# Attention biases gathered on the host, eight weight buffers, and norm chunks one group earlier in a two-layer diffusion backbone

## The chip, the cores and the metric

The kernel runs on one core of a Trainium2 chip. The metric is the device time of one execution in microseconds. The time before is the median of three runs, 2124.17 us (2123.88 to 2127.73).

A core has TensorE (PE in the profile; PEld are its weight loads), VectorE (DVE), ScalarE (ACT), GpSimd (POOL) and SyncE (SP), which here issues all DMAs. Each engine works through its own instructions in the order in which they were emitted, and semaphores order them between engines.

## The reference, cut to what matters

256 latent tokens and 256 context tokens of 1024 channels pass through two layers: half-step SwiGLU, a mixer, half-step SwiGLU, each after an RMSNorm with a learned shift and scale. The mixer projects to neighbourhood attention (8 heads), a Fourier mix and a windowed attention (8 heads, 2 key heads, a sink), and merges the three through gates. The second layer is computed for the latent tokens alone, where that suffices. The part that the change is about:

```python
dr_idx = key_rows - r[:, None] + NA_WIN_R - 1
dc_idx = jnp.clip(kcb - q_cols[..., None], -(NA_WIN_C - 1), NA_WIN_C - 1) + NA_WIN_C - 1
bias = bias_tab[:, dr_idx[:, None, None, :, None], dc_idx[None, :, :, None, :]]
...
s_loc = jnp.einsum('brcqhd,brcwkhd->bhrcqwk', qg, kb).astype(jnp.float32) * scale + bias[None]
s_loc = jnp.where(in_win[:, :, None, :], s_loc, NEG_INF)
```

The grid has 4 rows of 64 columns. A latent query sees all rows and 16 of the columns, with a bias by head, row distance and column distance, and besides all context keys without a bias. A context query sees the context keys alone.

## The kernel before, in words

Everything is held with channels along the 128 partitions. A product is one 128x128 weight block against a tile of 256 or 512 tokens, made of three matmuls in a reduced-precision form (`mm3`, L289 to L291): high half of the weights by high and low half of the tokens, then low half of the weights by the high half of the tokens. Order on every engine is the order of the program text (`manual_schedule`).

**Weights.** `Weights` streams 424 tiles of 8 products (128x1024, 512 KB) in a fixed order. A tile goes through a raw buffer (5 of them, loaded at L58), a high half written by ScalarE (`wh`, L67) and a low half, raw less high, written by VectorE or GpSimd (`wl`, L76). High and low halves share the pool `w` with 6 buffers, that is three tiles. `next` hands out one product. At the first product of tile n it emits the high half of tile n+2 (`ahead` is 2 after the first FFN group), and at the fifth the low half of n+2.

**Norms.** `Norm.chunks(k)` emits steps up to k+1. A step takes 128 channels of 256 tokens: VectorE multiplies (L206), ScalarE adds the shift and writes the high half (L208), and one step later VectorE writes the low half (L214). `first` in `ffn` is the first group of an FFN: it runs over k, emits `norm.chunks`, and multiplies the chunk with four weight blocks. With 512 tokens it does so in two passes of 256. The very first norm of the program (`norm.ready`) has steps of its own (`_first`, L221 to L229). The norm before the mixer is emitted from `fourier`, with its own calls. "The turn" is the place where one sublayer's last projection gives way to the next sublayer's norm and first group.

**Neighbourhood bias.** Eight tiles of the pool `act` (`nab`, two sets of four) hold biases for a pair of heads: 2 heads by 2 query halves, each 128 queries by 256 latent keys, with zeros behind for the 256 context keys (`memset` at L444). `na_bias_load` (L707) fills a set with eight DMAs that read a padded table in HBM with overlapping strides, in rows of 64 elements. `na_bias` (L711) adds the column mask on GpSimd, four adds a set. The set of pair 0 is loaded in `mix_loads`, at the end of the FFN before; it is masked, and pair 1 loaded, at the start of `mix`; the others follow at the end of each latent block (`after`, `bias_ahead`). `wa_mask` holds the windowed attention's band and 256 zeros, which also serve blocks without a mask.

**Attention.** `attention` runs a pipeline over blocks of four score tiles (128 queries by 512 keys, or 256 keys for context queries): scores (L726, L727), `weights` (L733: VectorE adds the mask and takes the row minimum of the negated sum; L735: ScalarE's exponential with its row sum), normalising (L752), transposes (L757), their split into high (L759, ScalarE) and low half (L764, VectorE), and the values (L775). Between the steps `fill` emits products of the projections that later blocks need, by due times (`DUES`). What these produce is split and moved between partitions by SyncE's DMAs: `stack` (L884) for queries and keys, L903 for the rotary embedding, with four or eight issues each. Of layer 0 there are 16 blocks, of layer 1 there are 8.

**The pool `act`** of 66 slots (2 KB a partition) holds all tiles of tokens: high and low halves, temporaries, scores. A tile's slot is reused when its last reader is done.

Of the kernel before, what the change touches and what calls it, by code (L numbers as in the profile page):

```python
# [14 lines left out]
KD = D // 128  # L15
DEPTH = 2
# [10 lines left out]
WINDOW = 128  # L27
BIAS_W = 2 * GRID_W - 1
O_NA_Q, O_NA_K, O_NA_V, O_FN, O_WA_Q, O_WA_K, O_WA_V, O_GATE = (
# [4 lines left out]
N_SUB = 424  # L34
N_ACT = 66
TAIL = 3
# [223 lines left out]
class Emit:  # L260
    def __init__(self, ctx, tc, d):
        self.tc, self.nc, self.d = tc, tc.nc, d
        pool = lambda name, bufs, **k: ctx.enter_context(tc.tile_pool(name=name, bufs=bufs, **k))
        self.const = pool("const", 1)
        self.act_p = pool("act", N_ACT)
        self.raw_p = pool("raw", 5)
        self.w_p = pool("w", 6)
        self.mod_p = pool("mod", 2)
        self.sm_p = pool("sm", 4)
        self.ps_p = pool("ps", 8, space=PSUM)  # L270
        self.W = Weights(self.nc, d["ws"], self.raw_p, self.w_p)
        self.mod = {}
# [90 lines left out]
    def setup(self):  # L363
# [55 lines left out]
        self.sin = c.tile([128, NLAT], F32, name="sin")  # L419
        self.na_mask = c.tile([128, NLAT], F32, name="na_mask")  # L420
        self.wa_mask = c.tile([128, 2, NT], F32, name="wa_mask")
        self.sink = c.tile([128, DEPTH, 4, 4], F32, name="sink")
# [3 lines left out]
    def setup_mix(self):  # L426
        nc, d = self.nc, self.d
        nc.sync.dma_start(out=self.g_fin, in_=d["g_final"])
        nc.sync.dma_start(out=self.cos, in_=d["cos"])
        nc.sync.dma_start(out=self.sin, in_=d["sin"])  # L430
        nc.sync.dma_start(out=self.na_mask, in_=d["na_mask"])
        nc.sync.dma_start(out=self.wa_mask, in_=d["wa_mask"])
        nc.sync.dma_start(out=self.sink, in_=d["sink"].partition_broadcast(128))
        yield
        nc.gpsimd.tensor_scalar(out=self.nsink, in0=self.sink, scalar1=-1.0, scalar2=None, op0=ALU.mult)

    def mix_loads(self, l):

        self.raw_dft = [self.tmp() for _ in range(2)]
        self.nc.sync.dma_start(out=self.raw_dft[0], in_=self.d["dft_n"])  # L440
        self.nc.sync.dma_start(out=self.raw_dft[1][:, :256], in_=self.d["dft_d"])
        self.nab = [[self.tmp() for _ in range(4)] for _ in range(2)]
        for t in self.nab[0] + self.nab[1]:
            self.nc.gpsimd.memset(t[:, NLAT:], 0.0)  # L444
        self.na_bias_load(l, 0)


# [60 lines left out]
    def ffn(self, l, which, n, norm, nxt):  # L508
# [12 lines left out]
        def first(passes):  # L521
# [3 lines left out]
            for vs in passes:  # L525
                lo, hi = 256 * vs[0], 256 * (vs[-1] + 1)
                for k in range(KD):
                    norm.chunks(vs[0] * KD + k)
                    if norm.ready:
# [164 lines left out]
    def na_bias_load(self, l, p):  # L694


        nc = self.nc
        tab = self.d["na_bias"]
        for i in range(4):
            t4 = self.nab[p % 2][i][:, :NLAT].rearrange("p (r c) -> p r c", c=GRID_W)  # L700
            hp, qt = divmod(i, 2)
            for r2 in range(2):
                first = WIN_R - 1 - (2 * qt + r2)
                off = ((l * 8 + 2 * p + hp) * GRID_W * (2 * WIN_R - 1) + first) * BIAS_W + GRID_W - 1
                src = bass.AP(tensor=tab.tensor, offset=tab.offset + off,
                              ap=[[(2 * WIN_R - 1) * BIAS_W - 1, GRID_W], [BIAS_W, ROWS], [1, GRID_W]])
                nc.sync.dma_start(out=t4[r2 * 64:r2 * 64 + 64], in_=src)  # L707

    def na_bias(self, p):
        for t in self.nab[p % 2]:  # L710
            self.nc.gpsimd.tensor_tensor(out=t[:, :NLAT], in0=t[:, :NLAT], in1=self.na_mask, op=ALU.add)  # L711

    def attention(self, makers, fill):
# [16 lines left out]
        def weights(b, i, ps):  # L730
            nk = len(b["kc"]) * 128
            e, nm = self.tmp(), b["nm"][:, i:i + 1]
            nc.vector.tensor_tensor_reduce(out=e[:, :nk], in0=ps, in1=b["mask"][i], scale=-1.0,  # L733
                                           scalar=b["init"][i], op0=ALU.add, op1=ALU.min, accum_out=nm)
# [109 lines left out]
    def mix(self, l, norm, nxt):  # L844
# [7 lines left out]
        if l == 0:  # L852
            next(self.mix_setup, None)
        self.na_bias(0)
        self.na_bias_load(l, 1)
        v_na = [self.split_heads(ps) for ps in self.project_rows(
# [143 lines left out]
        o_na, o_wa = [], []  # L1000
        zero = self.wa_mask[:, 0, NLAT:]

        def bias_ahead(p):
            self.na_bias(p)
            if p < 3:
                self.na_bias_load(l, p + 1)

# [14 lines left out]
        def na_block(p, lat):  # L1022
            def make():
                if lat:
                    o_na.append(self.tmp())
                return dict(q=ready(("nq", p)), k=ready(("nk", p)), q0=0 if lat else NLAT, o=o_na[p], sink=None,
                            kc=[0, 1, 2, 3] if lat else [2, 3], init=[3e38] * 4, left=left(o_na, p, lat),
                            after=(lambda: bias_ahead(p + 1)) if lat and p < 3 else None,
                            mask=self.nab[p % 2] if lat else [zero] * 4,
                            v=lambda kc, hp: v_na[kc][p // 2][:, (p % 2 * 2 + hp) * 128:(p % 2 * 2 + hp + 1) * 128])  # L1030
            return make

        def wa_block(p, lat):
            def make():
                if lat:
# [4 lines left out]
                            init=[self.nsink[:, l, p, i:i + 1] for i in range(4)],  # L1040
                            mask=[self.wa_mask[:, i % 2, :] for i in range(4)] if lat else [zero] * 4,
                            v=lambda kc, hp: v[kc // 2][:, (kc % 2 * 2 + hp) * 128:(kc % 2 * 2 + hp + 1) * 128])
# [87 lines left out]
def constants():  # L1130
# [6 lines left out]
    cos, sin = np.cos(ang).T, np.sin(ang).T  # L1137
    c = np.arange(GRID_W)
    start = np.clip(c - WIN_C // 2, 0, GRID_W - WIN_C)
    inside = (c[None] >= start[:, None]) & (c[None] < start[:, None] + WIN_C)  # L1140
    na = np.where(inside, 0.0, NEG).astype(f)
    band = np.where(np.abs(t[:, None] - t[None]) <= WINDOW, 0.0, NEG).astype(f).reshape(2, 128, NLAT)
    wa = np.concatenate([band, np.zeros((2, 128, NCTX), f)], -1).transpose(1, 0, 2)
    ang_n = 2 * np.pi * (np.outer(t, t) % NLAT) / NLAT
# [9 lines left out]
        "sin": np.concatenate([-sin, sin] * 2, 0),  # L1154
        "na_mask": np.tile(na, (2, ROWS)),
        "wa_mask": wa,
        "dft_n": dft_n,
# [4 lines left out]
def pack(inputs, order):  # L1162
# [67 lines left out]
```

## Time and profile before

| | |
|---|---|
| profiled execution | 2120.81 us, span 2119.0 us |
| three runs | 2124.17 us median (2123.88 to 2127.73) |
| mean granted TensorE clock | 0.992 |
| instructions | 29168 |
| ScalarE's high halves (L67) | 424 of 1056 ns |
| VectorE's low halves (L76) | 379 of 1254 ns |
| GpSimd's low halves (L76) | 45 of 2461 ns |
| bias loads (L707) | 64 issues of 64 KB, 2.7 us to landing |
| mask adds (L711) | 32, 25.2 us of GpSimd |
| HBM read | 305.99 MB, 145 GB/s over the span |

The profile is of one execution. Busy time counts an engine's instructions, not the waits of its queue. "Idle before" an instruction is the time that its engine stood, with what ended it. A wait for several things is put down to the one that came last. The share of busy time is an average over the program, so the stretch in which an engine stands is looked at by itself.

### The profile page before, as it was taken

To read this page: it belongs to the slowest core of one execution; us is meant where nothing else is said; L and a number is where in the kernel's file an instruction comes from. 1 tells how busy PE (TensorE), PEld (TensorE's weight loads), DVE (VectorE), ACT (ScalarE), POOL (GpSimd) and SP (SyncE) were. 2 spreads that over 40 slices of the span, in tenths; PEclk is the share of its full clock that TensorE was granted. 3 is DMA by queue.
4 is the path that set the end of the run, shared out by engine and by line. 5 is a ranking of instruction groups with operands and counts; after the bars stand their busy time and mean duration, and the time that the engine had idled before them with its cause. 6 is when DMAs were issued, how large, how long until landed. Compare 5 with 4: busy or idle time off the path is not lost. (4 is left out here: it accounts for less than half of the span.)

```text
span 2119.0 us, 29168 instructions
## 1 busy us (share of the span) xinstructions
PE 2050.9 (97%) x11193; PEld 1764.7 (83%) x11193; DVE 1283.7 (61%) x2035; ACT 848.5 (40%) x1362; POOL 355.7 (17%) x285
## 2 busy tenths in 40 slices
PE   7899999999999999999999989999999989999998
PEld 3688888878888888988888788888888878999998
DVE  6777776566675334687777465533336548566554
ACT  4422222345786222432222243222324458545443
POOL 4200000403441112300000220000012155330002
PEclk9999999999999999999999999999999999999999
DMA  7465566455532333466666545623344563554663
GB/s 271 139 199 182 196 199 212 124 152 144 136 85 73 100 92 98 150 186 193 199 189 200 186 143 186 199 90 100 99 112 145 145 177 110 160 179 153 186 181 109
DMA packets 119412, 327.05 MB, mean 154 GB/s; under 512 B 30692, under 2 KB 35940, under 8 KB 119272
## 3 DMA queue, kind: packets, MB, share of 16 engines
q1 hardware_dynamic: 119272, 325.18, 50.3%
q8 instruction: 88, 1.44, 0.3%
q14 instruction: 52, 0.43, 0.1%
HBM read 305.99 MB, written 1.05 MB: 145 GB/s over the span
## 5 line engine op out<-in xcount | busy, mean ns | idle before, releaser
L290 PE MATMUL ps<-act,wh 128*128 128x512 f32 (+1 forms) x3227 | 1120.9, 347 | 24.1 <-DVE act L229 13.6
L289 PE MATMUL ps<-act,wh 128*128 128x512 f32 (+1 forms) x3227 | 1121.3, 347 | 3.4 <-ACT act L298 1.9
L291 PE MATMUL ps<-act,wl 128*128 128x512 f32 (+1 forms) x3227 | 1118.9, 347 | 1.8 <-DVE wl L76 1.8
L67 ACT ACTIVATE wh<-raw 128x1024 fp32r<-128x1024 f32 x424 | 447.4, 1056 | 707.8 <-PE ps L290 573.7
L290 PEld LDWEIGHTS ps<-act,wh 128*128 128x128 f32 x3227 | 613.2, 190 | 101.8 <-DVE act L229 14.8
L289 PEld LDWEIGHTS ps<-act,wh 128*128 128x128 f32 x3227 | 613.1, 190 | 78.9 <-ACT act L298 2.5
L291 PEld LDWEIGHTS ps<-act,wl 128*128 128x128 f32 x3227 | 613.1, 190 | 77.9 <-DVE wl L76 2.9
L76 DVE TENSOR_TENSOR wl<-raw,wh 128x1024 fp32r<-128x1024 f32 x379 | 474.6, 1254 | 273.6 <-ACT wh L67 273.0
L311 DVE CUSTOM_DVE_ANT_0 dump<-ada,silu_row 128x1024 bf16<-128x1024 f32 x224 | 273.3, 1220 | 13.9 <-DMA ada<-in_w_ada 11.5
L298 ACT ACTIVATE act<-tmp 128x512 fp32r<-128x512 f32 (+1 forms) x122 | 66.9, 566 | 275.2 <-DVE tmp L516 261.8
L471 DVE SCALAR_TENSOR_TENSOR h<-ps,mod,h 128x256 f32<-128x256 f32 x136 | 61.7, 480 | 150.8 <-PE ps L291 150.8
L76 POOL TENSOR_TENSOR wl<-raw,wh 128x1024 fp32r<-128x1024 f32 x45 | 110.7, 2461 | 222.9 <-ACT wh L67 199.7
L454 POOL TENSOR_TENSOR tmp<-h 128x512 f32<-128x512 f32 (+1 forms) x7 | 11.6, 1661 | 782.3 <-DVE h L471 639.8
L516 DVE TENSOR_TENSOR tmp<-tmp,ps 128x512 f32<-128x512 f32 (+1 forms) x88 | 54.6, 621 | 112.1 <-PE ps L291 107.5
L299 DVE TENSOR_TENSOR act<-tmp,act 128x512 fp32r<-128x512 f32 (+1 forms) x122 | 74.3, 625 | 62.2 <-ACT act L298 62.2
L764 DVE TENSOR_TENSOR act<-ps,act 128x512 fp32r<-128x512 f32 x80 | 54.8, 685 | 35.8 <-ACT act L759 27.6
L735 ACT ACTIVATE tmp<-tmp,sm 128x512 f32<-128x512 f32 (+1 forms) x96 | 62.2, 648 | 32.8 <-DVE sm L733 31.5
L775 PE MATMUL ps<-act 128*128 128x256 f32 x320 | 63.0, 309 | 12.4 <-DVE act L764 11.2
L460 POOL TENSOR_TENSOR tmp<-h 128x256 f32<-128x256 f32 (+1 forms) x44 | 51.7, 1174 | 117.8 <-DVE h L471 112.9
L759 ACT ACTIVATE act<-ps 128x512 fp32r<-128x512 f32 x80 | 47.5, 593 | 39.9 <-PE ps L757 34.5
L444 POOL MEMSET tmp<- 128x256 f32 x16 | 4.8, 312 | 348.6 <-PE ps L291 347.9
L775 PEld LDWEIGHTS ps<-act 128*128 128x128 f32 x320 | 44.8, 189 | 17.5 <-DVE act L764 15.0
(110 smaller groups left out, 1372.8 us busy)
## 6 DMA issues: line engine op xcount, KB each, us to landing
raw<-in_ws SPq DMA_DIRECT2D x424, 512.0 KB, 3.7
ada<-in_w_ada SPq DMA_DIRECT2D x128, 512.0 KB, 3.9
act<-act SPq DMA_DIRECT2D x112, 128.0 KB, 2.3
tmp<-in_w_ada_sc SPq DMA_DIRECT2D x16, 256.0 KB, 5.2
tmp<-in_w_ada SPq DMA_DIRECT2D x16, 256.0 KB, 6.0
tmp<-in_na_bias SPq DMA_DIRECT2D x64, 64.0 KB, 2.7
h<-in_h SPq DMA_DIRECT2D x8, 256.0 KB, 5.2
act<-act SPq DMA_DIRECT2D x32, 64.0 KB, 2.0
```

The costliest lines, as they stand in the source:

```text
L67: self.nc.scalar.activation(out=wh, in_=self.raw[i], func=AF.Copy)
L76: self.lo_engine.tensor_tensor(out=wl, in0=self.raw.pop(i), in1=self.hi[i].bitcast(F32), op=ALU.subtract)
L289: mm(ps, lhsT=w[0], rhs=x[0], start=start, stop=False)
L290: mm(ps, lhsT=w[0], rhs=x[1], start=False, stop=False)
L291: mm(ps, lhsT=w[1], rhs=x[0], start=False, stop=stop)
L298: nc.scalar.activation(out=hi, in_=src, func=AF.Copy)
L299: nc.vector.tensor_tensor(out=lo, in0=src, in1=hi.bitcast(F32), op=ALU.subtract)
L311: self.nc.vector.tensor_tensor_reduce(out=self.dump[:, ks], in0=w, in1=self.silu_row[:, v, ks], scale=1.0, scalar=m if half else 0.0, op0= ...
L471: self.nc.vector.scalar_tensor_tensor(out=h, in0=ps, scalar=self.mod[l, g][:, v, j:j + 1], in1=h, op0=ALU.mult, op1=ALU.add)
L735: nc.scalar.activation(out=e[:, :nk], in_=e[:, :nk], func=AF.Exp, scale=-1.0, bias=nm, accum_out=b["sum"][:, i:i + 1])
L764: nc.vector.tensor_tensor(out=t[1], in0=ps, in1=t[0].bitcast(F32), op=ALU.subtract)
L775: nc.tensor.matmul(b["ps"][hp][:, :256], lhsT=v, rhs=t[j][:, cs], start=c == 0 and j == 0, stop=c == n - 1 and j == 1)
```

## The change

It does four things.

1. The biases are gathered on the host for each layer and pair of heads, with the column mask already in them, as 128 partitions by 4 tiles by 256 keys. A load is one DMA of 512 KB with 4 KB a partition.
2. One constant tile `masks` of 11 blocks of 256 keys takes the place of `nab`, `na_mask` and `wa_mask`: blocks 0 to 3 and 4 to 7 are the two bias sets, 8 and 9 the band of the windowed attention, 10 is zeros. A score tile of 512 keys reads its own block and block 10 with one strided view. The pairs 0 and 1 are both loaded in `mix_loads`, the pairs 2 and 3 after the blocks of 0 and 1. The adds of the column mask and the memsets are gone, and one memset of block 10 is added at the start.
3. The pool `w` has 8 buffers instead of 6, the pool `act` 60 instead of 66.
4. In `first`, `norm.chunks` is called for one k further, except in the program's first norm.

```diff
-N_ACT = 66
+N_ACT = 60
...
-        self.w_p = pool("w", 6)
+        self.w_p = pool("w", 8)
...
-        self.na_mask = c.tile([128, NLAT], F32, name="na_mask")
-        self.wa_mask = c.tile([128, 2, NT], F32, name="wa_mask")
+        self.masks = c.tile([128, 11, NLAT], F32, name="masks")
+        nc.gpsimd.memset(self.masks[:, 10, :], 0.0)
...
-        nc.sync.dma_start(out=self.na_mask, in_=d["na_mask"])
-        nc.sync.dma_start(out=self.wa_mask, in_=d["wa_mask"])
+        nc.sync.dma_start(out=self.masks[:, 8:10, :], in_=d["wa_mask"])
...
-        self.nab = [[self.tmp() for _ in range(4)] for _ in range(2)]
-        for t in self.nab[0] + self.nab[1]:
-            self.nc.gpsimd.memset(t[:, NLAT:], 0.0)
         self.na_bias_load(l, 0)
+        self.na_bias_load(l, 1)
...
-                    norm.chunks(vs[0] * KD + k)
+                    norm.chunks(vs[0] * KD + k + (not norm.ready))
...
     def na_bias_load(self, l, p):
...
+        self.nc.sync.dma_start(out=self.masks[:, p % 2 * 4:p % 2 * 4 + 4, :], in_=self.d["na_bias"][l, p])
...
-            nc.vector.tensor_tensor_reduce(out=e[:, :nk], in0=ps, in1=b["mask"][i], scale=-1.0,
+            m = b["mask"][i]
+            two = lambda t: t.rearrange("p (a k) -> p a k", k=NLAT)
+            blocks = (self.masks[:, m:m + 1, :] if nk == NLAT else self.masks[:, m:11:10 - m, :])
+            nc.vector.tensor_tensor_reduce(out=two(e[:, :nk]), in0=two(ps), in1=blocks, scale=-1.0,
                                            scalar=b["init"][i], op0=ALU.add, op1=ALU.min, accum_out=nm)
...
-        self.na_bias(0)
-        self.na_bias_load(l, 1)
...
-                            after=(lambda: bias_ahead(p + 1)) if lat and p < 3 else None,
-                            mask=self.nab[p % 2] if lat else [zero] * 4,
+                            after=(lambda: self.na_bias_load(l, p + 2)) if lat and p < 2 else None,
+                            mask=[p % 2 * 4 + i if lat else 10 for i in range(4)],
...
-                            mask=[self.wa_mask[:, i % 2, :] for i in range(4)] if lat else [zero] * 4,
+                            mask=[8 + i % 2 if lat else 10 for i in range(4)],
```

The rest of the diff is the packing of the inputs on the host, which is outside the time.

More of the change, by code (lines that the diff above doesn't have):

```diff
@@ L27 @@
 WINDOW = 128
-BIAS_W = 2 * GRID_W - 1
 O_NA_Q, O_NA_K, O_NA_V, O_FN, O_WA_Q, O_WA_K, O_WA_V, O_GATE = (
@@ L694, in na_bias_load @@
     def na_bias_load(self, l, p):
[L697 to L711, printed above, removed]
+        self.nc.sync.dma_start(out=self.masks[:, p % 2 * 4:p % 2 * 4 + 4, :], in_=self.d["na_bias"][l, p])
     def attention(self, makers, fill):
@@ L1000, in mix @@
         o_na, o_wa = [], []
[L1001 to L1006, printed above, removed]
         def split_out(o, p):
@@ L1137, in constants @@
     cos, sin = np.cos(ang).T, np.sin(ang).T
[L1138 to L1141, printed above, removed]
     band = np.where(np.abs(t[:, None] - t[None]) <= WINDOW, 0.0, NEG).astype(f).reshape(2, 128, NLAT)
-    wa = np.concatenate([band, np.zeros((2, 128, NCTX), f)], -1).transpose(1, 0, 2)
     ang_n = 2 * np.pi * (np.outer(t, t) % NLAT) / NLAT
@@ L1154, in constants @@
         "sin": np.concatenate([-sin, sin] * 2, 0),
-        "na_mask": np.tile(na, (2, ROWS)),
-        "wa_mask": wa,
+        "wa_mask": band.transpose(1, 0, 2),
         "dft_n": dft_n,
@@ L1175, in pack @@
     a["w_ada_sc"] = w["w_ada"][0, :, D:2 * D].reshape(KD, 128, 2, 512).transpose(2, 0, 1, 3)
-    pad = GRID_W - WIN_C
-    t = np.pad(w["na_bias"], ((0, 0), (0, 0), (0, 0), (pad, pad)))
-    a["na_bias"] = np.broadcast_to(t[:, :, None], t.shape[:2] + (GRID_W,) + t.shape[2:])
+    c, t = np.arange(GRID_W), np.arange(NLAT)
+    start = np.clip(c - WIN_C // 2, 0, GRID_W - WIN_C)
+    inside = (c[None] >= start[:, None]) & (c[None] < start[:, None] + WIN_C)
+    row, col = t // GRID_W, t % GRID_W
+    dr = row[None] - row[:, None] + WIN_R - 1
+    dc = np.clip(col[None] - col[:, None], 1 - WIN_C, WIN_C - 1) + WIN_C - 1
+    b = np.full((DEPTH, 8, NLAT, NLAT), NEG, np.float32)
+    inside = np.tile(inside, (ROWS, ROWS))
+    b[:, :, inside] = w["na_bias"][:, :, dr[inside], dc[inside]]
+    a["na_bias"] = b.reshape(DEPTH, 4, 2, 2, 128, NLAT).transpose(0, 1, 4, 2, 3, 5).reshape(DEPTH, 4, 128, 4, NLAT)
     s = w["wa_sink"]
@@ L1209 @@
     "c": (128, KD, 2), "b_ada": (128, DEPTH, 9, KD), "gains": (128, DEPTH, 3, 8), "g_final": (128, 8),
-    "na_bias": (DEPTH, 8, GRID_W, 2 * WIN_R - 1, BIAS_W), "sink": (DEPTH, 4, 4), "ident": (128, 128),
-    "cos": (128, NLAT), "sin": (128, NLAT), "na_mask": (128, NLAT), "wa_mask": (128, 2, NT),
+    "na_bias": (DEPTH, 4, 128, 4, NLAT), "sink": (DEPTH, 4, 4), "ident": (128, 128),
+    "cos": (128, NLAT), "sin": (128, NLAT), "wa_mask": (128, 2, NLAT),
     "dft_n": (128, 2 * NLAT), "dft_d": (128, 256),
```

## The prediction

> **What bounds the kernel now.** I read the page's busy times first, then a table of stretches, then what TensorE waited for, then the timeline at each place where it stood still.
>
> ```profile
> PE 2050.9 (97%) x11193; PEld 1764.7 (83%) x11193; DVE 1283.7 (61%) x2035; ACT 848.5 (40%) x1362; POOL 355.7 (17%) x285
> ```
>
> TensorE is busy 2050.9 us; nothing in this change removes a matmul, so only its idle time, and time at a lower clock, can be won. The stretches show where that lies (columns: length, then busy us and count by engine, granted clock, DMA share):
>
> ```profile
> core 0 of [0], span 2119.0 us
> core 0: us, PE busy (x) PEld busy (x) DVE busy (x) ACT busy (x) POOL busy (x), PEclk, DMA share, GB/s
> 20.00:75.00 55.00, 37.12 (x127) 23.15 (x128) 46.27 (x82) 25.49 (x44) 32.81 (x17) 0.84 0.48 176
> 415.00:446.00 31.00, 28.38 (x141) 22.43 (x140) 26.45 (x47) 18.49 (x29) 5.13 (x7) 1.00 0.54 155
> 510.00:690.00 180.00, 174.78 (x964) 147.76 (x963) 119.31 (x294) 131.47 (x316) 67.30 (x55) 1.00 0.40 107
> 1245.00:1278.00 33.00, 25.27 (x195) 23.93 (x196) 20.66 (x36) 15.06 (x23) 0.00 (x0) 1.00 0.48 144
> 1615.00:1632.00 17.00, 14.44 (x78) 11.69 (x77) 13.62 (x24) 8.60 (x15) 3.88 (x5) 1.00 0.46 135
> 1692.00:1726.00 34.00, 27.35 (x151) 23.36 (x150) 8.95 (x25) 13.65 (x27) 17.05 (x10) 0.95 0.86 216
> 1716.00:1722.00 6.00, 3.67 (x17) 3.47 (x18) 2.12 (x6) 2.68 (x5) 0.23 (x1) 0.72 1.04 313
> 1726.00:1800.00 74.00, 67.38 (x508) 62.52 (x509) 58.86 (x123) 59.65 (x142) 44.30 (x36) 1.00 0.41 116
> ```
>
> TensorE's idle time is length less busy: 17.9 us at the start (20 to 75), 2.6 at the turn into layer 0's mixer, 5.2 in its attention, 7.7 at the turn into layer 1's first FFN, 2.6 at the turn into layer 1's mixer, 6.7 and 6.6 in its attention. By the waits of TensorE the longest are:
>
> ```profile
> PE ps L290 <- DVE act L229: 13.6, 3, 6.2
> PE ps L775 <- DVE act L764: 11.2, 14, 2.9
> PE ps L290 <- DVE act L214: 7.5, 6, 1.4
> ```
>
> L229 is the first norm, which the change leaves alone. L214 (the low half of a norm chunk) and L764 (attention) are reached by it.
>
> **Part 1: eight weight buffers, and norm chunks one group earlier.** The six waits on L214 all lie between 1252 and 1275 and repeat exactly. One period:
>
> ```profile
> L67 ACT ACTIVATE wh<-raw 128x1024 fp32r<-128x1024 f32 x424 | 447.4, 1056 | 707.8 <-PE ps L290 573.7
> ...
> 1257.33 0.39 PE L290 MATMUL ps<-act,wh 128*128 128x256 f32 x1 [1.21 <-DVE act L214]
> ...
> 1258.52 1.06 ACT L67 ACTIVATE wh<-raw 128x1024 fp32r<-128x1024 f32 x1 [1.09 <-PE ps L290]
> ...
> 1259.61 1.23 DVE L76 TENSOR_TENSOR wl<-raw,wh 128x1024 fp32r<-128x1024 f32 x1 [1.55 <-ACT wh L67]
> 1260.76 0.48 DVE L206 SCALAR_TENSOR_TENSOR tmp<-ps,mod,h 128x256 f32<-128x256 f32 x1
> 1261.15 0.48 DVE L214 SCALAR_TENSOR_TENSOR act<-tmp,mod,act 128x256 fp32r<-128x256 f32 x1
> ...
> 1261.68 0.39 PE L290 MATMUL ps<-act,wh 128*128 128x256 f32 x1 [1.21 <-DVE act L214]
> ```
>
> This is a ring. TensorE resumes at 1257.33; 1.19 us later it ends a weight tile; only then may ScalarE write the high half (1.06 us) of the tile three ahead, because six buffers hold three tiles; VectorE makes the low half (1.15 us to the next start) and behind it, in order, the chunk whose L214 lets TensorE go on. Period 1261.68 - 1257.33 = 4.35 us, of which TensorE stands 1.21.
>
> With eight buffers the high half waits for the tile before, a whole tile earlier, so the ring spans two tiles: 4.35 / 2 = 2.2 us a tile against the 4.35 - 1.21 = 3.14 that TensorE needs. And the chunk is emitted one group (half a tile) earlier. Either breaks the ring. What is late next: VectorE has one low half (1.15) and two chunk pairs (1261.15 - 1260.76 = 0.39 each op, so 1.56) a tile, 2.7 us, below 3.14; ScalarE less. So TensorE binds again. I take 7.3 of the 7.5 us; ends 5 (a first wait stays while the new lead builds up) and 7.7 (all idle time of that row).
>
> Elsewhere ScalarE's 573.7 us of waiting for L290 go too, and I count that as nothing: TensorE has no gap there, so the conversion is hidden by a tile in hand. If that cover were gone it would show as waits on L67, which are not among the long ones. In layer 1's second FFN three chunks instead of two precede the first product: L206 and L214 more on VectorE, 0.8 us, behind the L214 that TensorE waits for first; a low half is queued behind them, so the ends are -0.8 and +0.2, and I take nothing.
>
> **Part 2: biases gathered on the host.** Each of eight loads (four head pairs, two layers) becomes one issue of 512 KB instead of eight of 64 KB:
>
> ```profile
> L707 SPq DMA_DIRECT2D tmp<-in_na_bias x64: 595/614/1261, 359.1 to 1721.5; - x64
> ...
> wa_mask<-in_wa_mask SPq DMA_DIRECT2D x1, 512.0 KB, 5.2
> ```
>
> SyncE's queue loses 56 x 0.614 = 34 us and the mask's one load. Most is hidden, since weights are loaded several tiles ahead; it matters where the queue itself is late. That is layer 1's attention:
>
> ```profile
> 1697.46 5.33 SPq L707 DMA_DIRECT2D tmp<-in_na_bias  x8
> ...
> 1706.67 7.82 SPq L884 DMA_DIRECT2D act<-act  x12
> ...
> 1715.42 0.69 DVE L764 TENSOR_TENSOR act<-ps,act 128x512 fp32r<-128x512 f32 x1 [7.37 <-DMA act<-act]
> ...
> 1716.00 0.60 ACT L759 ACTIVATE act<-ps 128x512 fp32r<-128x512 f32 x1 [4.96 <-DMA act<-act]
> ...
> 1716.16 0.62 PE L775 MATMUL ps<-act 128*128 128x256 f32 x3 [2.86 <-DVE act L764]
> 1718.95 1.12 PE L932 MATMUL ps<-ident,tmp 128*128 128x128 f32 x4 [2.17 <-ACT tmp L928]
> ```
>
> SyncE issues without a pause from 1697.46 to 1714.49. VectorE's and ScalarE's copies of the transposed weights wait for a slot that a head move (L884) still reads, and that move was issued behind the eight bias pieces. With one issue the moves go out up to 5.33 - 0.61 = 4.7 us earlier, more than the 2.86 us that TensorE stood, and the 2.17 on L928 (on ScalarE, behind the late L759) goes with it: 5.0 us. The moves are then behind one 512 KB transfer; the same bytes were ahead of them before. The DMA engines are busy 0.86 there, so part of the lead may be lost: ends 0 and 5.0.
>
> A load that follows a block still waits on SyncE for that block's last L733, because it overwrites the blocks that this one reads; the moves and the weights' issues (L58) are queued behind it, as they were. The second pair's load moves from the mixer's start to the place of the first, in the last projection of the FFN before: there it passes the weights' issues with 0.61 us, with four tiles loaded ahead, and in the mixer 4.9 us of SyncE go. TensorE waits for no raw tile at either place in the stretches above, so this is nothing, with ends -0.6 and 0.5.
>
> The clock: in 1716 to 1722 it was 0.72 on average, after these two gaps. TensorE was busy 3.67 us; at full clock that is about 3.67 x 0.72 = 2.6, so 1.0 us goes if the gaps go. [...]
>
> The remaining 6.6 us of idle time (1726 to 1800) come in small waits on L764 with VectorE and ScalarE busy 0.8 each. Less SyncE and less GpSimd work touches them in part: I take 1.0, ends -1 and 5. In layer 0's attention (5.2 idle) the first load's last pieces wait for the block's scores as the single one will, so I take 0.5, ends -2 and 3.
>
> **Part 3: GpSimd without the mask adds.**
>
> ```profile
> L711 POOL TENSOR_TENSOR tmp<-tmp,na_mask x32: 722/747/1180, 417.1 to 1735.5; 128x256 f32<-128x256 f32 x32
> ...
> 1615.34 3.55 POOL L711 TENSOR_TENSOR tmp<-tmp,na_mask 128x256 f32<-128x256 f32 x4
> ...
> 1617.74 0.56 DVE L214 SCALAR_TENSOR_TENSOR act<-tmp,mod,act 128x256 fp32r<-128x256 f32 x1
> 1618.22 2.88 DVE L76 TENSOR_TENSOR wl<-raw,wh 128x1024 fp32r<-128x1024 f32 x2
> ...
> 1620.02 0.50 PE L587 MATMUL ps<-wl,act 128*128 128x512 f32 x1 [2.11 <-DVE wl L76]
> ```
>
> At each turn into a mixer four adds run beside the chunks and the low half that TensorE waits for. VectorE's two low halves took 2.88 us; two spaced by 1.15 end after 1.15 + 1.23 = 2.38, so 0.5 is lost, and three L214 lost 0.08 each: 0.7 us in layer 1, about 0.5 in layer 0, 1.2 together; ends 0 and the whole idle time of both turns, 5.2.
>
> [...]
>
> The 16 memsets of the old tiles go; one new one of the same size joins the start, where GpSimd has other work in order: at most 0.3 us, taken as 0.
>
> **Part 4: what the new layout could cost.**
>
> ```profile
> L733 DVE CUSTOM_DVE_ANT_0 tmp<-ps,tmp 128x512 f32<-128x512 f32 x32 | 22.0, 687 | 24.5 <-PE ps L727 13.6 <-issue 10.8
> ...
> L299 DVE TENSOR_TENSOR act<-ps,act 128x512 fp32r<-128x512 f32 x16 | 11.0, 692 | 5.0 <-ACT act L298 4.8
> ```
>
> The score reduction (L733) now reads its mask as two blocks of 256 apart. No row shows this custom operation so; the nearest, L299 on split and permuted views, takes 692 ns for 512 elements against 687, so I take 0, with ends 0 and a second pass of 687 ns. The act pool has 60 slots instead of 66, but eight fewer tiles are held through the mixer, so two more are free there; in the FFNs six fewer, where no wait for a slot shows: 0, ends 0 and one stall like the 2.86.
>
> **Sum.** 7.3 + 5.0 + 1.0 + 1.0 + 0.5 + 1.2 = 16.0 us. The profiled execution took 2120.81 us, so 2104.8 like for like; the runs' median, 2124.17, lies 3.4 above, and against it the forecast is 2124.2 - 16.0 = 2108.2 us.
>
> **The rivals.**
> - *The ring alone breaks.* The DMA share of 0.86 speaks for it: moves land late however early they are issued, and layer 1's attention keeps its gaps. Gain 7.3 + 1.2 = 8.5: 2115.7 us.
> - *The mixer opens up.* VectorE and ScalarE are below 0.81 in 1726 to 1800, so its 6.6 may be mostly echoes of the queue. Then 5 there instead of 1, 3 in layer 0, 2 more at the turns: 2108.2 - 8.5 = 2099.7 us.
> - *A false wait.* The two-block read spans the blocks that are being loaded for the pair after; if dependencies are kept by the outer bounds, layer 1's third pair waits for the load issued just before it, 5.2 us as the 512 KB mask took. 2113.4 us. That the layer 0 blocks of context lie between speaks against more.
> - *Slower: the two-block reduction.* If each of the 64 takes a second pass, 64 x 0.69 = 44 us of VectorE. In layer 1 (32) it is on the way to L764 and TensorE, 22 us; in layer 0, busy 0.66, about half, 11: 2108.2 + 33 = 2141 us. It decides from about 0.33 us an instruction (16 / 48). L299 speaks against it.
> - *No change:* the gaps come back as waits on another engine's queue in the same places, 2120 to 2128 us. Against it: the ring's slack is worked out from rows.
>
> **How the numbers follow.** A measurement of this kernel can tell about 0.2% (4.2 us) from no change. Forecast 0.46, mixer opens 0.19, ring alone 0.17, false wait 0.05, no change 0.08, slower 0.05. Faster holds the first four, 0.87; same 0.08; slower 0.05. The range leaves out the last two and the edges of the others: 2098 to 2119.
>
> **What would show it.** Right: no wait on L214 between 1245 and 1278, and L67's waiting for L290 far below 573.7; one bias issue a load; L764 and L759 without waits for act moves, clock 1.00 from 1692 to 1800; no L711, L214 near 0.47 at mixer turns; L733 still near 687. Wrong: L733 above 1 us or waiting for the bias load; new waits of ScalarE for raw weights; the same gaps in layer 1's attention with SyncE idle.

## The result and the profile after

After: 2103.99 us, median of 4 runs (2101.61 to 2106.05); before, beside it, 2124.61 (2123.88 to 2127.73). The ratio is 0.990 with a 95% interval of 0.9883 to 0.9917. The forecast was 2108.2. One run in the experiments below, of the kernel with 64 act slots, took 4476.21 us and is left out of that kernel's row.

The profiled execution after took 2101.61 us against 2120.81. Code lines have moved: L67 is now L66, L76 L75, L206 L205, L214 L213, L229 L228, L290 L289, L587 L583, L588 L584, L707 L692, L726 L707, L727 L708, L733 L717, L752 L736, L757 L741, L759 L743, L764 L748, L775 L759, L884 L866, L928 L910, L932 L914. In the kernels with eight bias issues, the lines below the load stand three further down than in after.

Engine totals, two groups of instructions, and TensorE's waits after (waits: us in total, times, longest):

```profile
PE 2049.5 (98%) x11193; PEld 1764.6 (84%) x11193; DVE 1282.1 (61%) x2035; ACT 838.4 (40%) x1362; POOL 340.6 (16%) x238
```

```profile
L66 ACT ACTIVATE wh<-raw 128x1024 fp32r<-128x1024 f32 x424 | 436.4, 1050 | 318.4 <-PE ps L289 281.7 <-issue 18.7 <-PE ps L583 4.4
...
L717 DVE CUSTOM_DVE_ANT_1 tmp<-ps,masks 128x512 f32<-128x512 f32 x32 | 22.0, 688 | 24.1 <-PE ps L708 24.0
```

```profile
PE ps L289 <- DVE act L228: 9.8, 2, 5.8
PE ps L759 <- DVE act L748: 9.2, 14, 2.2
...
PE ps L583 <- DVE wl L75: 2.1, 2, 1.3
PE ps L290 <- DVE wl L75: 1.8, 3, 0.9
PE ps L584 <- DVE act L213: 1.7, 3, 1.2
```

The busy time of TensorE is the same to 1.4 us; the time came out of its pauses. The waits on the low half of a norm chunk at layer 1's FFN turn (7.5 us, six times, on L214, now L213) are gone from the list. ScalarE stands 281.7 us for TensorE instead of 573.7. The reduction that reads its mask as two blocks takes 688 ns; it was 687. It waits for scores only, never for a bias load.

The stretches that answer to those of before:

```profile
core 0: us, PE busy (x) PEld busy (x) DVE busy (x) ACT busy (x) POOL busy (x), PEclk, DMA share, GB/s
415.00:446.00 31.00, 28.87 (x141) 22.89 (x140) 26.33 (x46) 18.82 (x31) 1.44 (x3) 1.00 0.53 161
510.00:690.00 180.00, 174.93 (x961) 147.53 (x960) 117.66 (x292) 131.42 (x317) 60.42 (x46) 1.00 0.39 105
1241.60:1266.60 25.00, 24.66 (x194) 23.66 (x195) 20.70 (x36) 14.24 (x23) 0.00 (x0) 1.00 0.61 179
1603.00:1620.00 17.00, 15.15 (x85) 12.41 (x84) 13.48 (x25) 9.21 (x16) 1.13 (x2) 1.00 0.49 153
1675.00:1708.00 33.00, 30.19 (x175) 26.06 (x174) 17.59 (x31) 15.82 (x31) 15.86 (x7) 1.00 0.86 249
1708.00:1782.00 74.00, 67.04 (x507) 62.12 (x506) 58.24 (x123) 59.08 (x142) 41.22 (x32) 1.00 0.41 117
```

At layer 1's FFN turn 0.3 us of idle time are left of 7.7. In layer 1's attention (the last two rows) the clock is 1.00 throughout, and TensorE idles 2.8 us in the first stretch instead of 6.7, but still 7.0 in the second. One period of the former ring, VectorE's and ScalarE's rows:

```profile
1250.60 1.23 DVE L75 TENSOR_TENSOR wl<-raw,wh 128x1024 fp32r<-128x1024 f32 x1 [0.35 <-ACT wh L66]
...
1251.74 0.48 DVE L205 SCALAR_TENSOR_TENSOR tmp<-ps,mod,h 128x256 f32<-128x256 f32 x1
...
1252.13 0.47 DVE L213 SCALAR_TENSOR_TENSOR act<-tmp,mod,act 128x256 fp32r<-128x256 f32 x1
...
1252.67 1.04 ACT L66 ACTIVATE wh<-raw 128x1024 fp32r<-128x1024 f32 x1
```

The high half at 1252.67 waits for nothing; in the row of before it carried 1.09 us of waiting for TensorE. The next high halves follow at 1255.82 and 1258.97, a period of 3.15 us, against the 3.14 that the prediction worked out for TensorE alone.

**Where the 19 us went.** Both kernels have 11193 matmuls in their traces, in the same order, so the start of each in one trace can be set against its start in the other. For instance matmul 5873 starts at 1245.14 before and 1241.74 after, and matmul 6068 at 1278.04 and 1266.87: 11.17 less 3.40 is 7.8 us won at layer 1's FFN turn. All stretches so:

| stretch (us of before) | after less before | forecast |
|---|---|---|
| start, to 76 | -0.6 | 0 |
| turn into layer 0's mixer, 415 to 446 | -0.6 | -0.5 |
| layer 0's mixer and attention, to 690 | 0.0 | -0.5 |
| layer 0's second FFN, to 1180 | -1.0 | 0 |
| its last product, to 1195 | -1.3 | 0 |
| turn into layer 1's first FFN, to 1278 | -7.8 | -7.3 |
| turn into layer 1's mixer, 1614 to 1640 | -0.7 | -0.7 |
| layer 1's attention, 1640 to 1800 | -6.0 | -7.0 |
| layer 1's second FFN and end | -1.1 | 0 |
| sum (rows are rounded) | -19.0 | -16.0 |

Here and in the tables below, such numbers come from one execution of each kernel. The start moves by -1.2 and +0.4 us when nothing but the number of `act` slots changes (after with 58 instead of 60, before with 67 instead of 66), so the -0.6 there is not shown to be an effect of the change.

### The profile page after: what moved, and what is told of

Same layout as the page of the kernel before. It is cut to its first block, busy times and chain, and to the rows that moved or that the text cites. A ratio compares the mean times of both kernels' runs of the same rounds, so it can differ in the third digit from the quotient of the medians.

```text
span 2099.8 us, 28967 instructions
## 1 busy us (share of the span) xinstructions
PE 2049.5 (98%) x11193; PEld 1764.6 (84%) x11193; DVE 1282.1 (61%) x2035; ACT 838.4 (40%) x1362; POOL 340.6 (16%) x238
## 3 DMA queue, kind: packets, MB, share of 16 engines
q8 instruction: 88, 1.44, 0.3%
## 5 line engine op out<-in xcount | busy, mean ns | idle before, releaser
L289 PE MATMUL ps<-act,wh 128*128 128x512 f32 (+1 forms) x3227 | 1121.4, 348 | 10.6 <-DVE act L228 9.8
L290 PE MATMUL ps<-act,wl 128*128 128x512 f32 (+1 forms) x3227 | 1120.1, 347 | 1.8 <-DVE wl L75 1.8
L289 PEld LDWEIGHTS ps<-act,wh 128*128 128x128 f32 x3227 | 613.6, 190 | 86.7 <-DVE act L228 10.5
L290 PEld LDWEIGHTS ps<-act,wl 128*128 128x128 f32 x3227 | 613.7, 190 | 78.1 <-DVE wl L75 2.6
L66 ACT ACTIVATE wh<-raw 128x1024 fp32r<-128x1024 f32 x424 | 436.4, 1050 | 318.4 <-PE ps L289 281.7
L75 DVE TENSOR_TENSOR wl<-raw,wh 128x1024 fp32r<-128x1024 f32 x379 | 473.3, 1261 | 102.6 <-ACT wh L66 102.6
L512 DVE TENSOR_TENSOR tmp<-tmp,ps 128x512 f32<-128x512 f32 (+1 forms) x88 | 54.6, 621 | 208.6 <-PE ps L290 203.1
L75 POOL TENSOR_TENSOR wl<-raw,wh 128x1024 fp32r<-128x1024 f32 x45 | 111.4, 2477 | 225.9 <-ACT wh L66 215.1
L298 DVE TENSOR_TENSOR act<-tmp,act 128x512 fp32r<-128x512 f32 (+1 forms) x122 | 74.3, 626 | 61.0 <-ACT act L297 61.0
L511 ACT ACTIVATE tmp<-ps 128x512 f32<-128x512 f32 (+1 forms) x88 | 47.8, 543 | 123.4 <-PE ps L290 122.8
L456 POOL TENSOR_TENSOR tmp<-h 128x256 f32<-128x256 f32 (+1 forms) x44 | 64.4, 1463 | 107.0 <-DVE h L467 104.4
L748 DVE TENSOR_TENSOR act<-ps,act 128x512 fp32r<-128x512 f32 x80 | 54.9, 686 | 30.1 <-ACT act L743 27.5
L759 PE MATMUL ps<-act 128*128 128x256 f32 x320 | 62.5, 308 | 10.3 <-DVE act L748 9.2
L743 ACT ACTIVATE act<-ps 128x512 fp32r<-128x512 f32 x80 | 47.5, 594 | 46.2 <-PE ps L741 44.7
L1070 DVE TENSOR_TENSOR tmp<-tmp,ps 128x512 f32<-128x512 f32 (+1 forms) x48 | 26.0, 551 | 62.3 <-PE ps L290 61.0
```

The lines of the kernel that those rows point to most:

```text
L66: self.nc.scalar.activation(out=wh, in_=self.raw[i], func=AF.Copy)
L75: self.lo_engine.tensor_tensor(out=wl, in0=self.raw.pop(i), in1=self.hi[i].bitcast(F32), op=ALU.subtract)
L289: mm(ps, lhsT=w[0], rhs=x[1], start=False, stop=False)
L290: mm(ps, lhsT=w[1], rhs=x[0], start=False, stop=stop)
L298: nc.vector.tensor_tensor(out=lo, in0=src, in1=hi.bitcast(F32), op=ALU.subtract)
L456: nc.gpsimd.tensor_tensor(out=sq, in0=h, in1=h, op=ALU.mult)
```

## The experiments

All kernels, each against runs of the kernel before on the same chip (its medians there were 2122.65, 2122.34 and 2121.77 for the first four, the next four and the last four rows):

| kernel | median us (range) | ratio (95%) |
|---|---|---|
| after, 6 weight buffers | 2104.92 (2104.36 to 2106.18) | 0.9914 (0.9899 to 0.9929) |
| after, no earlier chunk | 2105.79 (2104.28 to 2106.57) | 0.9916 (0.9903 to 0.9929) |
| after, neither | 2113.14 (2111.31 to 2113.96) | 0.9950 (0.9936 to 0.9963) |
| before, with both alone, 62 act slots | 2132.86 (2128.09 to 2133.65) | 1.0042 (1.0028 to 1.0055) |
| after, eight bias issues | 2104.90 (2102.20 to 2109.54) | 0.9921 (0.9908 to 0.9935) |
| after, 58 act slots | 2110.45 (2106.57 to 2111.57) | 0.9938 (0.9925 to 0.9952) |
| after, GpSimd adds again | 2105.44 (2104.02 to 2107.91) | 0.9923 (0.9910 to 0.9935) |
| after, 6 weight buffers, 64 act slots | 2105.33 (2103.35 to 2106.18) | 0.9920 (0.9906 to 0.9933) |
| before, 67 act slots | 2121.51 (2119.40 to 2123.46) | 1.0000 (0.9991 to 1.0009) |
| after, eight issues and 58 slots | 2113.28 (2111.12 to 2117.09) | 0.9964 (0.9949 to 0.9980) |
| after, chunks earlier at mixer turns too | 2103.46 (2101.14 to 2105.27) | 0.9916 (0.9902 to 0.9929) |
| the same with weights prepared 3 ahead | 2098.95 (2098.12 to 2100.50) | 0.9896 (0.9882 to 0.9909) |

### The ring: one half, the other, neither

```diff
-        self.w_p = pool("w", 8)
+        self.w_p = pool("w", 6)
```

> The changed kernel with six weight buffers again, norm chunks still one group ahead. Theory (either part breaks the ring): the ring's 4.35 us now spans one and a half tiles, 2.9 us a tile, against 2.87 to 3.14 us of TensorE, so the waits on the norm's low half at layer 1's first FFN stay under 1 us in sum and the time is that of the changed kernel, 2104 to 2106 us. Rival (only the buffers break it): six waits of about 1.2 us come back there, 2111 to 2112 us.

```diff
-                    norm.chunks(vs[0] * KD + k + (not norm.ready))
+                    norm.chunks(vs[0] * KD + k)
```

> The changed kernel with norm chunks at their old place, eight weight buffers kept. Theory (either part breaks the ring): 2.2 us a tile, no waits on the norm's low half, 2104 to 2105 us. Rival (only the lead breaks it): six waits of about 1.2 us come back, 2111 to 2112 us.

Both edits together:

> The changed kernel with six weight buffers and norm chunks at their old place: the bias part alone. Theory: the ring is back with its six waits, 7.7 us, so 2111 to 2113 us, and layer 1's attention keeps its gain of 6 us against the kernel before. Rival (the gain in layer 1's attention comes from the weight buffers, which leave ScalarE free earlier): the stall of 2.9 us and the clock dip there come back as well, 2117 to 2119 us.

With either half of the part the time stays within 2 us of after; with neither it is 2113.1, which is 8.2 above the one and 7.4 above the other, on one chip. TensorE's wait with neither, then the only wait on a chunk that is left at this turn without the earlier chunk, then ScalarE's row with six buffers and the earlier chunk:

```profile
PE ps L289 <- DVE act L213: 7.4, 6, 1.3
```

```profile
1250.46 0.39 PE L289 MATMUL ps<-act,wh 128*128 128x256 f32 x1 [1.34 <-DVE act L213]
```

```profile
L66 ACT ACTIVATE wh<-raw 128x1024 fp32r<-128x1024 f32 x424 | 447.3, 1056 | 700.6 <-PE ps L289 556.1 <-issue 87.8 <-ACT wh L66 18.6
```

The six waits come back when both halves are undone, and only then. Layer 1's attention keeps 5.5 of its 6.0 us with neither half (1640 to 1800, matmul starts against before), so that gain does not come from the weight buffers. The second row is the wait of which the prediction said that "a first wait stays while the new lead builds up": buffers alone leave it, the earlier chunk removes it. The third row tells a reader what not to conclude: with six buffers ScalarE stands 556 us for TensorE, as before the change, yet the time is that of after. A long wait on an engine off the critical path was no sign of the ring; the six waits of TensorE were.

This part is worth 9.1 us between the medians (2113.14 less 2103.99, which were not timed side by side), more than the 7.8 of the turn. The rest is in the second FFNs. In the trace with neither, the first group of layer 0's second FFN starts and ends as before; with either half, and in after, it is 0.5 to 0.8 us shorter, and that of layer 1 0.5 to 0.7. Before, TensorE made pauses of some 0.3 to 0.4 us there, once a tile:

```profile
887.37 0.28 PE L289 MATMUL ps<-act,wh 128*128 128x256 f32 x1
887.77 0.39 PE L290 MATMUL ps<-act,wh 128*128 128x256 f32 x1
...
890.62 0.28 PE L289 MATMUL ps<-act,wh 128*128 128x256 f32 x1
890.92 0.39 PE L290 MATMUL ps<-act,wh 128*128 128x256 f32 x1
```

Matmuls of this form start 0.12 apart; these are 0.40 and 0.30 apart, and the ones behind them 0.23 and 0.22 (kernel before). The kernel with neither half has the same spacings at the same matmuls, and after has 0.12 there. The pauses do not appear in the list of TensorE's waits.

### The ring's edit alone, on the kernel before

```diff
-N_ACT = 66
+N_ACT = 62
...
-        self.w_p = pool("w", 6)
+        self.w_p = pool("w", 8)
...
-                    norm.chunks(vs[0] * KD + k)
+                    norm.chunks(vs[0] * KD + k + (not norm.ready))
```

> The kernel before with eight weight buffers and the lead of the norm chunks, its biases and masks as they were; the act pool has 62 slots instead of 66 to make room. Theory (parts add up): the ring's 7.7 us and the 1.4 us at the end of layer 0's last FFN half go, 2115 to 2116 us, and the 2.9 us stall in layer 1's attention stays. Rival (weight buffers free ScalarE in the attention too): 2109 to 2112 us. Second rival (four slots fewer in the mixer cost more waits for slots there): above 2118 us, with longer waits for act moves.

It is slower than before: 2132.86. The FFN turn gained the same 7.8 us, but layer 0's mixer and attention lost 7.7 (446 to 690) and layer 1's attention 18.4 (1640 to 1800). The kernel before holds eight slots for bias tiles through the mixer, so 62 leave 54 where before had 58 and after has 60. VectorE's and ScalarE's waits for a slot that a head move still reads, and TensorE's behind them, in this kernel:

```profile
DVE tmp L733 <- DMA act<-act: 13.6, 1, 13.6
...
ACT act L759 <- DMA act<-act: 17.4, 2, 9.0
```

```profile
1711.14 0.58 PE L289 MATMUL ps<-act,wh 128*128 128x256 f32 x1 [5.96 <-ACT wh L67]
...
1722.04 1.01 PE L775 MATMUL ps<-act 128*128 128x256 f32 x3 [3.51 <-DVE act L764]
```

VectorE's L733 stands 13.6 us for a slot, ScalarE then waits for it and makes its high halves late, and TensorE waits for these. In 1700 to 1735 the mean granted clock is 0.75, so a part of the loss is time at a lower clock. Slots in the pool `act` thus have a price, which the prediction set at nothing.

### The attention: issues, slots or adds

```diff
-        self.nc.sync.dma_start(out=self.masks[:, p % 2 * 4:p % 2 * 4 + 4, :], in_=self.d["na_bias"][l, p])
+        for i in range(4):
+            for r2 in range(2):
+                s = slice(r2 * 64, r2 * 64 + 64)
+                self.nc.sync.dma_start(out=self.masks[s, p % 2 * 4 + i, :], in_=self.d["na_bias"][l, p, s, i, :])
```

> The changed kernel, each bias load in eight issues of 64 KB again (rows of 1 KB), nothing else. Theory (the stall in layer 1's attention came from SyncE issuing eight pieces ahead of the head moves): the moves are 4 to 5 us later there, the waits for act moves on VectorE and ScalarE come back with 2 to 5 us of TensorE and the clock dip, 2107 to 2110 us. Rival (it came from two slots too few in the mixer's act pool): the time stays at 2104 to 2105 us.

```diff
-N_ACT = 60
+N_ACT = 58
```

> The changed kernel with 58 act slots, which leaves the mixer as many free slots as the kernel before had (66 less eight bias tiles). Rival (slots): the 2.9 us stall and the clock dip of layer 1's attention come back, 2109 us and more. Theory (SyncE's issues): at most 1.5 us slower than the changed kernel, 2104 to 2106 us, since the moves that free the slots go out early.

Both:

> The changed kernel with both 58 act slots and eight issues a bias load. New theory (slots alone): as with 58 slots and one issue, 2109 to 2112 us. Either-or (the late moves need both few slots and many issues to stall TensorE near 1700): the 2.9 us stall and the clock dip come back on top, 2113 to 2117 us.

These kernels and after make a square. The first three columns of numbers are matmul starts against the kernel before, as above; the fourth is the sum of VectorE's and ScalarE's waits on head moves; the last the median.

| | 1640 to 1700 | 1700 to 1720 | 1720 to 1800 | waits on moves | median |
|---|---|---|---|---|---|
| before (eight issues, 58 free) | 0 | 0 | 0 | 21.1 | 2121.8 to 2124.6 |
| one issue, 60 slots (after) | -1.1 | -4.4 | -0.5 | 2.9 | 2103.99 |
| eight issues, 60 slots | -1.1 | -3.6 | +2.1 | 13.2 | 2104.90 |
| one issue, 58 slots | 0.0 | -4.4 | +7.3 | 13.4 | 2110.45 |
| eight issues, 58 slots | -0.7 | -0.1 | +3.6 | 26.6 | 2113.28 |

The waits behind the fourth column, after, and then with both edits (where a last one, of 0.4 us on L720, makes up the sum):

```profile
DVE act L748 <- DMA act<-act: 2.6, 1, 2.6
ACT act L891 <- DMA act<-act: 0.3, 1, 0.3
```

```profile
ACT act L746 <- DMA act<-act: 10.3, 1, 10.3
DVE act L751 <- DMA act<-act: 9.0, 2, 8.0
DVE act L876 <- DMA act<-act: 6.9, 1, 6.9
```

And SyncE and TensorE of the kernel with both edits at the place of the old stall:

```profile
1685.91 5.34 SPq L695 DMA_DIRECT2D masks<-in_na_bias  x8
1691.35 3.16 SPq L869 DMA_DIRECT2D act<-act  x4
...
1704.68 1.01 PE L762 MATMUL ps<-act 128*128 128x256 f32 x3 [2.81 <-DVE act L751]
1707.45 1.11 PE L917 MATMUL ps<-ident,tmp 128*128 128x128 f32 x4 [1.76 <-ACT tmp L913]
```

This is the 2.86 and 2.17 of before, brought back with its chain: bias pieces ahead of the moves, the copy late, TensorE late. But it takes both edits. The prediction's chain is real, and one issue is enough to remove that stall at 58 slots (-0.1 to -4.4). Two slots more remove most of it as well, with all eight issues left in (-0.1 to -3.6): the wait on the copy goes, but the one on L928 (L910 in after, L913 here) stays at 2.18 where after has 1.44. After has both, and the second adds under 1 us there. The kernel with both edits keeps all the rest of the change, the biases gathered on the host, the new places of the loads, GpSimd without adds and the ring's edits, and its stall is that of before to 0.1 us. So none of these removed it. One issue also has rows of 4 KB where the eight have 1 KB; the two were not run apart.

The third column needs care, since a lower clock comes and goes in it. After and the kernel with six weight buffers, which has one issue and 60 slots too, pause at the same matmul for nearly the same time. Each one's pause, and the clock behind it, first after, then six weight buffers:

```profile
1756.70 0.62 PE L759 MATMUL ps<-act 128*128 128x256 f32 x3 [2.20 <-DVE act L748]
...
1755.00:1765.00 10.00, 8.30 (x63) 7.82 (x64) 8.63 (x19) 7.23 (x18) 5.35 (x4) 1.00 0.41 131
```

```profile
1758.33 0.73 PE L759 MATMUL ps<-act 128*128 128x256 f32 x3 [2.29 <-DVE act L748]
...
1758.70:1762.10 3.40, 3.40 (x17) 3.28 (x16) 3.37 (x7) 1.26 (x4) 1.89 (x1) 0.50 0.60 161
```

With six weight buffers 3.4 us at a granted clock of 0.50 follow, and the next 87 matmuls take 1.6 us longer than after's. The same happens behind this pause with eight issues (at 1760.0), with 58 slots and one issue (1763.9) and with GpSimd's adds (1761.4); it does not happen with neither half of the ring or without the earlier chunk, whose pauses are 2.26 and 2.22 us. So it is not shown that any of these edits causes it, and 1.6 us in this column tell nothing of issues or slots.

Over the whole of layer 1's attention the rows add up to -6.0, -2.6, +2.9 and +2.8. Without the 1.6 us, which the second and third have, they are -6.0, -4.2, +1.3 and +2.8: two slots are then worth 7.3 us with one issue and 7.0 with eight, and one issue 1.8 us with 60 slots and 1.5 with 58. The medians give 6.5 and 8.4 for the slots, 0.9 and 2.8 for the issue. They were not timed on one chip, and the ratios of after and of eight issues overlap, so the issue's share over the whole attention is an estimate. On any of these counts the slots are the larger term. A sum of waits does not give the time: 13.2 and 13.4 us of waits lie in kernels 5.5 us apart.

With one issue and 58 slots, three pauses that after has too have grown, from 1.38, 1.26 and 1.12 us to 2.43, 2.15 and 2.59 (at 1719.6, 1735.6 and 1751.2). The mean granted clock is 0.50 from 1719.5 to 1722.9 and from 1736.6 to 1740.0, behind the first two. The growth is 3.4 us, and the matmuls behind these two pauses take 2.7 us longer than after's; together that is most of the 7.3. Before, with as many free, shows none of this loss, and what spares it there isn't settled. The first of these pauses:

```profile
1718.80 0.69 DVE L748 TENSOR_TENSOR act<-ps,act 128x512 fp32r<-128x512 f32 x1 [1.42 <-POOL tmp L888]
...
1719.55 1.01 PE L759 MATMUL ps<-act 128*128 128x256 f32 x3 [2.43 <-DVE act L748]
```

Here VectorE stands behind GpSimd's rotary work, not behind a move.

Two more runs on the slots:

> The kernel before with 67 act slots instead of 66, nothing else (68 do not fit): 59 are free in its mixer, one more than it had. New theory (layer 1's attention is short of act slots, and the two more of the change are its gain there): the waits of VectorE and ScalarE for act moves near 1700 to 1716 shrink and a part of the 6 us goes, 2116 to 2121 us against 2122.3. Old theory (SyncE's bias issues): no change, 2122 to 2124 us, the 2.9 us stall stays.

> The changed kernel with six weight buffers, whose room goes to four more act slots (64): the lead alone breaks the ring. If slots are what the attention lacks: the waits for act moves at 513 and in layer 1's attention shrink, 2100 to 2103 us. If they are not: as the changed kernel with six weight buffers, 2104 to 2105 us.

One slot more in the kernel before gives nothing: 1.0000 (0.9991 to 1.0009). The 2.86 on the copy goes, but the wait on L932 grows from 2.17 to 3.32:

```profile
1717.07 1.11 PE L932 MATMUL ps<-ident,tmp 128*128 128x128 f32 x4 [3.32 <-ACT tmp L928]
```

From 1716 to 1722 the mean granted clock is 0.50, where before had 0.72. Its 1700 to 1720 is 1.8 shorter and its 1720 to 1800 is 2.4 longer. With 64 slots in after (and six weight buffers, to make the room) nothing is won over 60 either: 0.9920 beside 0.9914 for six buffers with 60, intervals that overlap. By these times slots are a step between 58 and 60 in the new layout, and not a slope that goes on.

### GpSimd's adds

GpSimd adds the block of zeros to each bias block, at the places and in the number of before, so its work is back and the output is the same.

```diff
+    def na_bias(self, p):
+        for i in range(4):
+            m = self.masks[:, p % 2 * 4 + i, :]
+            self.nc.gpsimd.tensor_tensor(out=m, in0=m, in1=self.masks[:, 10, :], op=ALU.add)
```

> The changed kernel with the 32 GpSimd adds back at their old places; they add the block of zeros to the bias blocks, so the result is the same. Theory (adds slow VectorE's two-input instructions, by what the trace showed): at the two turns into a mixer TensorE waits 0.5 to 0.8 us longer, 1.2 in sum, and the attention hardly changes: 2105 to 2106 us. Rival (GpSimd and VectorE block each other wholly): 3 us and more, 2107 us or above.

Layer 1's mixer turn with the adds, and then the row of after:

```profile
1606.97 3.55 POOL L697 TENSOR_TENSOR masks<-masks 128x256 f32<-128x256 f32 x4
...
1609.86 2.88 DVE L75 TENSOR_TENSOR wl<-raw,wh 128x1024 fp32r<-128x1024 f32 x2
...
1611.66 0.50 PE L583 MATMUL ps<-wl,act 128*128 128x512 f32 x1 [2.11 <-DVE wl L75]
```

```profile
1608.04 0.50 PE L583 MATMUL ps<-wl,act 128*128 128x512 f32 x1 [1.30 <-DVE wl L75]
```

The adds cost 0.8 us here, to the digit the 2.11 of before, with the same 2.88 us for the two low halves (2.43 in after) and 0.56 for each of three L213. At layer 0's turn they cost 0.4. The median is 1.5 us above after, which the intervals can't tell from nothing. That "the attention hardly changes" is not borne out by this one profile: 446 to 690 and 1720 to 1800 are each 2.7 us longer than after's. The first holds a wait of 2.84 us for a head move, where after has 1.56, with 3.4 us at half clock behind it, and the second the half clock near 1761. The kernel of the next section, which has no adds, waits 3.63 us for that move, so whether the adds have a part in this is open.

### A better version

```diff
-            norm.chunks(k)
+            norm.chunks(k + 1)
...
-            norm.chunks(KD + k)
+            norm.chunks(KD + k + 1)
```

> The changed kernel with norm chunks one group ahead at the turns into the mixers too. Theory: the waits on the norm's low half at the end of both context passes go, 1.2 us in layer 0 and 0.5 in layer 1, and little else: 2102 to 2103 us. Rival (two chunks more on VectorE ahead of the weights' low halves at the turn's start): the waits on the low half, 0.8 and 1.3 us, grow by up to 0.8 each, 2104 to 2106 us.

With this and:

```diff
-            W.ahead = 2
+            W.ahead = 3
```

> As the run with the lead at the mixers, and the weights' halves made three tiles ahead instead of two, which eight buffers hold. Theory: the waits on weights' low halves at the turns (0.8, 0.9, 1.3 and 0.8 us) go, since a whole tile more is in hand, and the ring, now over one and a half tiles again, stays open: 2098 to 2101 us. Rival (the conversion again waits for TensorE, and queues ScalarE's other work behind it in the attention): no gain or up to 4 us lost there, 2102 to 2107 us.

The earlier chunks at the mixer turns alone give nothing that the time can tell (0.9916, 0.9902 to 0.9929). In the profile the two turns are 0.3 and 1.1 us shorter than after's, and TensorE's waits on L213 fall from 1.7 to 0.7 us, but 446 to 690 is 3.6 longer. At the turns TensorE still waits for low halves of the weights (0.77 and 1.30 us) that the chunks don't move. With weights prepared three tiles ahead, which eight buffers allow, the waits on `wl` go from the list of TensorE's waits, and the norms' sums (L175) take part of their place:

```profile
PE ps L175 <- ACT tmp L462: 3.8, 6, 0.9
...
PE ps L584 <- DVE act L213: 0.7, 1, 0.7
```

After had 3.9 us on `wl` and 1.4 on L175. The kernel is 4.5 us below the one without `ahead` 3, on one chip and with no overlap of their runs (2098.12 to 2100.50 against 2101.14 to 2105.27). It is the fastest that ran: 5.0 below the median of after. After was not timed beside it, though, and the ratios to before are 0.9896 and 0.990, so a gain over after isn't shown.

## Why the prediction was right

The time, 2104.0, lies in the range and 4.2 below the forecast; the gain is 20.6 us by medians, 19.2 by the profiles, where 16.0 was worked out. No rival describes it: the ring alone would have been 2115.7, the mixer did not open (7.0 us of idle time after where 6.6 were), and no load made a score wait. That the sum came so near is partly luck: the start (0.6) and the last product of layer 0's second FFN (1.3), which no term covers, make up for the attentions, which gave 1.5 less than was taken.

**Part 1: right in mechanism, short in size.** 7.3 was taken for the turn and 7.8 came, above the upper end of 7.7: all of the row's idle time and a little more. The period is the worked-out one, and "either breaks the ring" is what the square of runs shows. The step that failed is the part's last paragraph: for layer 1's second FFN "I take nothing", with -0.8 to +0.2 as ends, and layer 0's was not named. Their first groups gave 0.7 and 0.8, so the ring's edits are worth 9.3 us by stretches and 9.1 by medians. Counting ScalarE's 573.7 us as nothing was right. Taking their fall as a sign of being right was not: with six buffers they stay (556.1), and the gain is there all the same.

**Part 2: right sum, a cause that is only half of it.** Layer 1's attention gave 6.0 of the 7.0: 4.4 for the stall and its time at half clock (0.50 from 1719 to 1721 in before), where 5.0 and 1.0 stood, 1.1 ahead of it and 0.5 behind, where 1.0 stood. That no half clock followed the pause at 1756.7 in this execution is luck, worth 1.6 us. The gap on the copy went. L932's 2.17 became 1.44, and the wait behind it, on L741, is still there:

```profile
1702.08 0.66 PE L914 MATMUL ps<-ident,tmp 128*128 128x128 f32 x4 [1.44 <-ACT tmp L910]
1707.74 0.66 PE L741 MATMUL ps<-ident,tmp 128*128 128x128 f32 x4 [1.37 <-ACT tmp L882]
```

The step that failed is the attribution: "that move was issued behind the eight bias pieces", therefore one issue. The row said that VectorE waits for a slot until a move has read it. Such a wait has two cures, an earlier move and another slot, and the change brought both. With eight issues put back the old stall's stretch loses 0.8 of its 4.4. Part 4 had the other cure in hand ("two more are free there") and took it at 0, with one stall like the 2.86 as the worst end. The runs price the two slots at some 7 us (6.5 and 8.4 by medians), on the gain's side, and the one issue at some 1.5 to 1.8 (0.9 and 2.8), where 5.0 was put down to the issue alone.

Layer 0's attention was taken at 0.5 and gave 0.0, with the mixer's start inside the stretch. The last product of layer 0's second FFN gave 1.3 that no step had. It is in other kernels too, in part or in whole: -0.3 with neither half of the ring, -1.4 in before with 67 slots, so it isn't this change's alone. In before TensorE waits 1.06 us for ScalarE's L298 there; what takes that wait away is open.

**Part 3: right.** 1.2 us was worked out for two turns, 1.3 came, and the run with the adds put 0.4 and 0.8 back. Three L213 beside the adds took 0.56 us each, where those of after take 0.47. The 2 us more at the turns that the second rival adds up are shown by no run: the two turns gave 0.6 and 0.7 us in all.

**Part 4: the costs at nothing.** The reduction costs 688 ns instead of 687. Rival four, 2141 us, hung on that one number and fell with it. The slots are told of above.

## What to carry to other kernels

When the profile says that a copy waits for a transfer into the same pool, ask for both cures, the earlier transfer and the further buffer, and test them crosswise. Here each hid the other: undoing either alone left most of the stall away, and only undoing both brought it back. Before a pause is blamed for a loss, look at the granted clock behind it, since the same pause came with a granted clock of 0.50 behind it in one kernel (2.29 us) and of 1.00 in another (2.20 us). This ring across in-order engines was broken by two more buffers or by emitting the late link earlier, and either was enough; the waits of ScalarE, off the path, didn't tell whether it was broken, and TensorE's period did. Buffers are taken from somewhere: the same edits that are worth 9 us here made the kernel before 10 us slower, where four slots went with them.

## What was not expected of the hardware

Two of VectorE's scalings of the exponentials (L736, 128x512) took 4.91 us beside GpSimd's low halves, where two without them took 0.88; other VectorE instructions lost far less beside GpSimd's adds. In after, VectorE beside the low halves and without them, and then GpSimd:

```profile
1691.80 4.91 DVE L736 TENSOR_SCALAR tmp<-tmp,sm 128x512 f32<-128x512 f32 x2
...
1708.23 0.88 DVE L736 TENSOR_SCALAR tmp<-tmp,sm 128x512 f32<-128x512 f32 x2
```

```profile
1689.12 7.30 POOL L75 TENSOR_TENSOR wl<-raw,wh 128x1024 fp32r<-128x1024 f32 x3 [2.18 <-ACT wh L66]
```

Each of the first two took about as long as the GpSimd instruction beside it (4.91 / 2 = 2.46 us, and 7.30 / 3 = 2.43 us). In the run with the adds, VectorE's two low halves took 2.88 us, where they take 2.43 in after, and L213 took 0.56 us instead of 0.47. L205 kept its 0.47 us beside the adds. What makes L736 so much slower beside GpSimd is not shown. TensorE has no wait on L736's results there, so it cost nothing in this place.

The other surprise is the clock behind the pause before the last stretch of layer 1's attention. The granted clock fell to 0.50 for 3.4 us behind pauses of 2.20 to 2.29 us in four kernels, and stayed at 1.00 behind pauses of 2.20 to 2.49 us in five. What decides between the two is not shown.
